# Down projection in scaled float16 pairs but for its last two rows, the sums of w_down taken under the output projection, seven PSUM banks in turn

## The chip, the cores and the metric

The kernel runs on one core of a Trainium2 chip. The metric is the device time of one execution in microseconds. A profiled execution gives a trace beside it: for each engine (PE is TensorE, PEld its weight loads, DVE is VectorE, ACT is ScalarE, POOL is GpSimd, SP is SyncE, which issues most DMAs) when each instruction ran, what it waited for, and what the DMA queues moved.

## The reference, cut to what matters

One decoder layer: modulation, a combined input projection, attention with forget gates beside a short gated convolution, an output projection, and a feed-forward part with a causal convolution of three taps. The end of it is what the change touches:

```python
x = x + g1 * (mixed @ w_out)
h2 = rmsnorm(x, norm2_g) * (1 + sc2) + sh2
u = causal_dwconv(h2 @ w_up, ffn_conv_w)
u_gate, u_val = jnp.split(u, 2, axis=-1)
y = (jax.nn.silu(u_gate) * u_val) @ w_down
return x + g2 * y
```

The sequence has 2048 tokens, the model width is 1024, the feed-forward width 2816, which is 22 rows of 128. All inputs and the output are float32.

## The kernel before

A float32 product is made as three products of pairs: each operand is split into a high part and a remainder, and high x high, high x low and low x high are added up in a PSUM bank of 512 columns (`mm3`, line 142). In the attention's end, the output projection and the up projection the parts are float16 of values that were first scaled by a power of two; in the input projection and the down projection they are f32r, a float32 with a shortened mantissa, and no scale is needed.

The stages that matter here, in order of time:

- **Output projection** (`mixed`). 64 steps n = 8 b + i: four blocks Q of 512 tokens, two column halves hf each, eight rows i of `w_out`. `prepare` makes the float16 pairs some steps ahead: a weight pair wp (in the first block) and a pair mp of the mixed activations, each with a scaled copy on ACT (line 778) and a remainder on DVE (779). At a block's first half each mp frees the buffer `src` of its raw tile, and `load_mixed` queues the load of the next block's tile into it on SP. A half block ends with four DVE readouts (826), which add x and free the four accumulator banks. A second chain, `early`, is run one piece per step under steps 17 and up, but for the last of each eight: `norm2` of blocks 0 and 1 (squares on ACT, 1108; the inverse root and the scaling on DVE, 1111 to 1115; then per column four PE transposes into the one bank of `ps_n`, line 1091, which ACT reads out, 1093, with pairs and differences after it), and then the weights of the first up row.
- **Up projection** (`up`), two halves of 1024 tokens, 22 rows i each. A row is a Strassen-like scheme of seven products of 12 matmuls (line 1250) in three banks X, Y, Z: X with o11; Y with os2; X with o12; Z with os1; Y with os3; Z with os4; Y with o22. X after o11 is copied to p1 on ACT (1295). DVE makes u2 = p1 + Y after os2 and u3 = p1 + Y after os3 (1156); the next product into Y may not start before the sum has read it. `up_weights(i + 1)` loads the next weights, scales both tiles on ACT (1176) and makes their differences and pairs. `finish`, called `last` one row later, makes the three taps of the convolution (one on ACT, 1258, two on DVE, 1263), silu (1272) and the gated product (1275), which goes to DRAM as `y_sc`.
- **Down projection** (`down`), also once per half: for each of four blocks n (token block and column half) 22 rows i. `load_pair` brings 512 columns of y and of `w_down` into one raw tile of 1024 columns, `split_pair` makes hi on ACT (1221) and lo on DVE (1222), two to three rows ahead of PE. The last two rows are multiplied together per token tile, and four readouts (1067, 1068) close the block. The four accumulators come from `ps_d`, which has four banks; `ps_u` has three more and `ps_n` one. In the first half `down` also runs `last`, `norm2` of blocks 2 and 3 and the first weights of the second up stage as a side chain, every second row.

`K(...)` pins instructions to the order in which the code issues them, and each engine works strictly in that order; PE, DVE, ACT and SP each have their own. SP's queue holds the loads in program order, so a load whose buffer is not free yet keeps back those behind it.

Of the kernel before, what the change touches and what calls it, by code (L numbers as in the profile page):

```python
# [9 lines left out]
F32 = mybir.dt.float32  # L10
# [30 lines left out]
LINES = 528  # L41
NTEMP = 7


@with_exitstack
def kernel(
# [679 lines left out]
    def halves(tiles):  # L726

        return [[t[:, n * 512 : (n + 1) * 512] for t in tiles] for n in range(2)]
# [4 lines left out]
    def load_out(n):  # L733
# [10 lines left out]
        )  # L744

    def out_scales(pool):
# [12 lines left out]
        K(T.matmul(pt[:, 0:2], lhsT=ones[0:2, :], rhs=gm, start=True, stop=True))  # L759
        bits = osc.bitcast(I32)  # L760
        K(V.tensor_scalar(osc, pt[:, 0:2], 2.0**-40, 2.0**60, op0=ALU.max, op1=ALU.min))
        K(V.tensor_scalar(bits, bits, 0x7F800000, None, op0=ALU.bitwise_and))
        K(V.reciprocal(osc, osc))
        K(V.tensor_scalar(bits, bits, 0x7F800000, None, op0=ALU.bitwise_and))
        K(V.tensor_scalar(osc, osc, 16384.0, None, op0=ALU.mult))
        K(V.tensor_tensor(oinv, osc[:, 0:1], osc[:, 1:2], op=ALU.mult))
        K(V.reciprocal(oinv, oinv))
        yield
# [284 lines left out]
    with ExitStack() as ph:  # L1053
# [10 lines left out]
        def add_gated(acc, gate, src, dst):  # L1064

            g = temp()
            K(V.tensor_tensor(g, acc, gate, op=ALU.mult))  # L1067
            K(V.tensor_tensor(src, src, g, op=ALU.add))
            nc.sync.dma_start(dst, src)

        bt = {}

# [23 lines left out]
        def norm2(Q):  # L1096

            if Q == 0:
                fp.tile([P, 96], F32, name="rim2")
            ss = fp.tile([P, 16], F32, tag="ss", name="ss", bufs=2)[:, 0:4]  # L1100
# [117 lines left out]

        def split_pair(raw):
            hi, lo = pair_tiles()  # L1220
            K(A.activation(hi, raw, AF.Copy))  # L1221
            K(V.tensor_tensor(lo, raw, hi.bitcast(F32), op=ALU.subtract))  # L1222
            y, wd = halves((hi, lo))
            return (*y, *wd)

        raws, pairs = {}, {}

        def first_pairs(hv):

            for i in range(3):  # L1230
                raws[4 * hv, i] = load_pair(4 * hv, i)
            yield
            for i in range(3):
                pairs[4 * hv, i] = split_pair(raws.pop((4 * hv, i)))
                yield
            while True:
                yield

        def up(hv):
# [25 lines left out]
            def finish(i, p1, Y, gate, val, yg):  # L1265
# [14 lines left out]
            last = None  # L1280
            for i in range(NPAIR):
                o11, o12, os2, os4, os3, o22, os1 = ops
# [12 lines left out]
                K(A.activation(p1, X, AF.Copy))  # L1295
                if last:
# [25 lines left out]
                keep_halo(gate, i)  # L1322
                next(wts)
                product(Y, o22, "t4", False)
                last = finish(i, p1, Y, gate, val, yg)
            return last

        def down(hv, side):

            todo = [(n, i) for n in range(4 * hv, 4 * hv + 4) for i in range(NPAIR)]  # L1330
            loaded = split = 3
            for e, (n, i) in enumerate(todo):
                Q, n0 = n // 2, n % 2 * 512
                rows = [slice((Q * 4 + t) * P, (Q * 4 + t + 1) * P) for t in range(4)]
                while split < min(e + 3, len(todo)):
                    if loaded == split:
                        raws[todo[loaded]] = load_pair(*todo[loaded])
                        loaded += 1
                    pairs[todo[split]] = split_pair(raws.pop(todo[split]))
                    split += 1  # L1340
# [24 lines left out]
        weights = first_weights()  # L1365
        early = chain(steps[0], (None for _ in range(1)), steps[1], weights)
        for n, _ in enumerate(mix, 8):
            if n >= 17 and n % 8 != 7:
                next(early, None)
# [33 lines left out]
```

## Time and profile before

| what | us |
|---|---|
| timed runs, median of 3 (2454.68 to 2456.41) | 2456.35 |
| the profiled execution's own time | 2452.39 |
| its span, first to last instruction | 2450.4 |
| PE busy in the span | 2361.1 (96%) |
| DVE busy | 1782.4 (73%) |
| ACT busy | 1257.3 (51%) |
| POOL busy | 361.3 (15%) |

Reading it: the mean granted TensorE clock of the span is 0.995. A matmul's length in the trace is modelled and overlaps the next one's, so the spacing of a run of matmuls (time over count) tells their rate, and the lengths of single ones don't. Shares of busy time are means over stages with different limits; the stages are looked at one by one.

### The profile page before, as it was taken

What the parts mean: (1) busy time and instruction counts of PE and PEld (TensorE: products, weight loads), DVE (VectorE), ACT (ScalarE), POOL (GpSimd) and SP (SyncE); (2) the same over time, 40 slices, a digit from 0 to 9 for tenths busy, and PEclk for the clock granted to TensorE, in tenths of its full rate; (3) what the DMA queues carried; (4) which work ended last, traced back from release to release, by engine and by line L of the source; (5) the groups of instructions that cost most, each with busy time, mean ns of one, the idle gap of its engine ahead of it and who ended that gap; (6) DMA issues with size and microseconds to landing.
All of it is one profiled execution on the core that took longest, in us unless ns stands there. A gap on an engine that the chain in (4) does not pass through costs nothing.

```text
span 2450.4 us, 38339 instructions
## 1 busy us (share of the span) xinstructions
PE 2361.1 (96%) x14419; PEld 1586.0 (65%) x14419; DVE 1782.4 (73%) x3325; ACT 1257.3 (51%) x2016; POOL 361.3 (15%) x302
## 2 busy tenths in 40 slices
PE   4999999999899888999999999999999999999999
PEld 4988788888677666444444444688864444448887
DVE  7567884442799888556888889757768888885554
ACT  3533453221588887343656565555545556554333
POOL 4210111101567785001000000000000000000000
PEclk9999999999999999999999999999999999999999
DMA  8435686543599987524222222676742222236775
GB/s 241 148 119 128 173 243 191 158 134 95 117 183 174 218 166 160 185 104 155 78 86 87 86 86 76 202 240 226 230 145 80 93 86 86 86 103 211 228 228 184
DMA packets 428707, 368.70 MB, mean 150 GB/s; under 512 B 184209, under 2 KB 327913, under 8 KB 427497
## 3 DMA queue, kind: packets, MB, share of 16 engines
q1 hardware_dynamic: 421400, 349.40, 50.4%
q10 hardware_dynamic: 4752, 8.46, 1.0%
q0 software_dynamic: 2368, 8.39, 0.9%
q8 instruction: 113, 1.85, 0.3%
q14 instruction: 74, 0.60, 0.1%
HBM read 267.54 MB, written 65.08 MB: 136 GB/s over the span
## 4 chain that ended last, share of the span: by engine, by line
PE 79%; DVE 7%; issue 5%; DMA 4%; ACT 3%; POOL 2%; SPq 1%; ACTq 0%; DVEq 0%; POOLq 0%
PE acc L1250 33%; PE acc L142 26%; PE pr L142 11%; PE pv L142 2%; DMA far<-wide 2%; PE pt L934 1%; DVE near L941 1%; PE ps L873 1%; DVE s_t L897 1%; PE ps L874 1%; PE po L970 1%; DVE acc L235 1%; PE po L972 1%; PE po L971 1%; POOL wide L926 1%
## 5 line engine op out<-in xcount | busy, mean ns | idle before, releaser
L1250 PEld LDWEIGHTS <-pair 128*128 128x128 f16 x3696 | 361.6, 98 | 436.1 <-issue 0.3
L1250 PE MATMUL acc<-t,pair 128*128 128x512 f16 x2112 | 477.4, 379 | 0.0
L1250 PE MATMUL acc<-b,pair 128*128 128x512 f16 x1584 | 363.4, 379 | 0.0
L1222 DVE TENSOR_TENSOR lo<-raw,hi 128x1024 fp32r<-128x1024 f32 x176 | 212.0, 1223 | 153.8 <-ACT hi L1221 153.5
L142 PE MATMUL acc<-hi 128*128 128x512 f32 x704 | 276.8, 393 | 1.6 <-DVE t L1067 1.6
L142 PE MATMUL acc<-lo,hi 128*128 128x512 f32 x704 | 274.3, 390 | 0.5 <-DVE lo L1222 0.5
L142 PE MATMUL acc<-hi,lo 128*128 128x512 f32 x704 | 274.1, 389 | 0.0
L1221 ACT ACTIVATE hi<-raw 128x1024 fp32r<-128x1024 f32 x176 | 182.3, 1055 | 178.7 <-PE acc L142 137.8
L1263 DVE SCALAR_TENSOR_TENSOR w<-w,fcw,w 128x1024 f32<-128x1024 f32 x176 | 226.2, 1285 | 34.6 <-ACT w L1258 25.3
L1074 ACT ACTIVATE pair<-raw 128x1024 f16<-128x1024 f32 x132 | 138.3, 1048 | 68.5 <-DVE raw L1157 68.5
L142 PE MATMUL acc<-wp,mp 128*128 128x512 f16 x768 | 171.1, 382 | 1.0 <-DVE raw L826 1.0
L1258 ACT ACTIVATE w<-w,fcw 128x1024 f32<-128x1024 f32 x88 | 100.7, 1144 | 130.6 <-DVE w L1156 130.6
L914 ACT ACTIVATE s_t<-s_t,nb,cst 128x2048 f32<-128x2048 f32 (+15 forms) x128 | 164.7, 1288 | 5.2 <-ACT nb L911 0.4
L1077 DVE TENSOR_TENSOR pair<-raw,pair 128x1024 f16<-128x1024 f32 x132 | 160.9, 1219 | 4.7 <-ACT pair L1074 4.7
L142 PE MATMUL pr<-hh,wh 128*128 128x512 f32 x384 | 153.3, 399 | 0.0
L142 PEld LDWEIGHTS acc<-hi 128*128 128x128 f32 x704 | 132.2, 188 | 31.3 <-DVE t L1067 4.4
L605 ACT ACTIVATE wx<-wx 128x512 f32<-128x512 f32 x88 | 55.6, 632 | 187.4 <-DMA wx<-in_w_up_dram 163.0
L142 PE MATMUL pr<-hl,wh 128*128 128x512 f32 x384 | 151.0, 393 | 0.0
L142 PE MATMUL pr<-hh,wl 128*128 128x512 f32 x384 | 150.7, 392 | 0.0
L142 PEld LDWEIGHTS acc<-hi,lo 128*128 128x128 f32 x704 | 132.1, 188 | 27.9
L142 PEld LDWEIGHTS acc<-lo,hi 128*128 128x128 f32 x704 | 132.2, 188 | 27.7 <-DVE lo L1222 1.1
L926 POOL TENSOR_TENSOR wide<-s_t,wide 128x1024 f16<-128x1024 f32 x64 | 136.8, 2137 | 5.3
(298 smaller groups left out, 4711.8 us busy)
## 6 DMA issues: line engine op xcount, KB each, us to landing
raw<-in_w_up_dram SPq DMA_DIRECT2D x88, 512.0 KB, 3.7
raw<-y_sc SPq DMA_DIRECT2D x176, 256.0 KB, 4.0
raw<-in_w_down_dram SPq DMA_DIRECT2D x176, 256.0 KB, 5.6
wx<-in_w_up_dram SPq DMA_DIRECT2D x88, 256.0 KB, 2.9
y_sc<-w SPq DMA_DIRECT2D x44, 512.0 KB, 2.6
wm<-in_w_ada_dram SPq DMA_DIRECT2D x128, 128.0 KB, 2.9
wr<-in_w_in_dram SPq DMA_DIRECT2D x40, 256.0 KB, 3.4
x_t<-in_x_dram SPq DMA_DIRECT2D x16, 512.0 KB, 5.4
```

What stands on the lines that cost most here:

```text
L142: ins = T.matmul(acc, lhsT=a, rhs=b, start=st, stop=sp)
L235: K(V.scalar_tensor_tensor(a, wa[:, k, :], cact[:, k : k + 1], a, op0=ALU.mult, op1=ALU.add))
L605: K(A.activation(t, t, AF.Abs, accum_out=l1[:, n : n + 1]))
L914: K(A.activation(cols, cols, AF.Exp, bias=nb[:, p : p + 1], scale=qk[:, 4:5], accum_out=un["l"][:, p : p + 1]))
L926: K(G.tensor_tensor(wide[:, 1, :], s_t[:, WB * P : WU], wide[:, 0, :], op=ALU.subtract))
L1074: K(A.activation(hi, raw, AF.Copy))
L1077: K(V.tensor_tensor(lo, raw, hi, op=ALU.subtract))
L1221: K(A.activation(hi, raw, AF.Copy))
L1222: K(V.tensor_tensor(lo, raw, hi.bitcast(F32), op=ALU.subtract))
L1250: K(T.matmul(acc, lhsT=a, rhs=b, start=st, stop=sp, skip_group_check=True))
L1258: K(A.activation(y, u[:, 0:1024], AF.Copy, scale=fcw[:, ct : ct + 1]))
L1263: K(V.scalar_tensor_tensor(y, u[:, m : m + 1024], fcw[:, m * 44 + ct : m * 44 + ct + 1], y, op0=ALU.mult, op1=ALU.add))
```

## The change

Lines are those of the program after the change where code is new, and of before in the rows of before.

1. The down projection's pairs become float16 for the first 20 of 22 rows (`LAST = 20`). y and w_down get one scale each, a power of two from their largest sums, and the readout multiplies by the inverse. The last two rows stay f32r, since y's scale must be known before their values are.

```diff
+        def split_pair(e, i, raw):
+            scales = big["rim"][:, 46:48]
+            if i < LAST:
+                t = fq.tile([P, 2048], F16, tag=("hi", "lo")[e % 2], name="yw", bufs=4)
+                parts = [[t[:, (2 * n + m) * 512 : (2 * n + m + 1) * 512] for m in range(2)] for n in range(2)]
+            else:
+                parts = halves(pair_tiles())
+            for n, (hi, lo) in enumerate(parts):
+                half, sc = raw[:, n * 512 : (n + 1) * 512], scales[:, n : n + 1]
+                K(A.activation(hi, half, AF.Copy, scale=sc))
+                K(V.scalar_tensor_tensor(lo, half, sc, hi if i < LAST else hi.bitcast(F32), op0=ALU.mult, op1=ALU.subtract))
+            return (*parts[0], *parts[1])
...
-            K(V.tensor_tensor(g, acc, gate, op=ALU.mult))
+            K(V.scalar_tensor_tensor(g, acc, big["rim"][:, 48:49], gate, op0=ALU.mult, op1=ALU.mult))
```

2. Largest sums of w_down: 22 loads of 128x1024 on SP and 22 sums of absolute values on ACT, one of each per two steps of the output projection, the sum one step behind its load. They take the two buffers `first`, which the first up weights used. Largest sums of y: one sum on ACT per up row below 20, one row later.

```diff
+        def weight_sums(i):
+            t = fp.tile([P, 1024], F32, tag="first", name="wd", bufs=2)
+            K(nc.sync.dma_start(t, w_down[i * P : (i + 1) * P, :]))
+            return lambda: K(A.activation(t, t, AF.Abs, accum_out=big["rim"][:, 20 + i : 21 + i]))
...
         for n, _ in enumerate(mix, 8):
+            if sums_of:
+                sums_of.pop()()
+            if n % 2 and 9 <= n < 9 + 2 * NPAIR:
+                if n == 9:
+                    big["rim"] = fp.tile([P, 96], F32, name="rim2")
+                sums_of.append(weight_sums((n - 9) // 2))
...
+                if i < LAST:
+                    junk = fp.tile([P, D], BF16, tag="t2", name="junk", bufs=NTEMP)
+                    mags.append(lambda: K(A.activation(junk, yv, AF.Abs, accum_out=big["rim"][:, i : i + 1])))
```

3. The scales are made in the last up row, in `first_pairs`: two DVE reductions, a PE transpose, two small DVE steps, a PE matmul and seven small DVE steps (`powers_of_two`, which `out_scales` now calls too). Two pairs instead of three are split before the down projection starts. In every up row p1's copy is now issued ahead of the next weights' scaling.

```diff
                 product(X, o11, "b11", True)
+                p1 = temp()
+                K(A.activation(p1, X, AF.Copy))
                 wts = up_weights(i + 1) if i + 1 < NPAIR else first_pairs(hv)
                 ops = next(wts)
-                p1 = temp()
-                K(A.activation(p1, X, AF.Copy))
...
-            for i in range(3):
-                pairs[4 * hv, i] = split_pair(raws.pop((4 * hv, i)))
+            K(V.tensor_reduce(om[:, 0:1], rim[:, 0:LAST], axis=AX.X, op=ALU.max))
+            K(V.tensor_reduce(om[:, 1:2], rim[:, 20 : 20 + NPAIR], axis=AX.X, op=ALU.max))
+            yield
+            pt = ps_n.tile([P, 512], F32, tag="n", name="pt")
+            K(T.transpose(pt[0:2, 0:P], om, ident))
...
+            K(T.matmul(pt[:, 0:2], lhsT=ones[0:2, :], rhs=gm, start=True, stop=True))
+            powers_of_two(pt[:, 0:2], sc, inv)
...
+            for i in range(2):
+                pairs[4 * hv, i] = split_pair(i, i, raws.pop((4 * hv, i)))
```

4. The accumulators of the down projection go round seven banks, the four of `ps_d` and the three of `ps_u`.

```diff
-                    acc = [ps_d.tile([P, 512], F32, tag="d", name="acc") for _ in range(4)]
+                    acc = []
+                    for c in range(16 * hv + 4 * (n - 4 * hv), 16 * hv + 4 * (n - 4 * hv) + 4):
+                        low_bank = (c - 16 * hv) % 7 < 4
+                        acc.append((ps_d if low_bank else ps_u).tile([P, 512], F32, tag="d" if low_bank else "u", name="acc"))
```

What this moves, as the built programs have it. First ACT in the middle of an up stage, one row before (pair is a weight pair, raw the next weights, t<-acc is p1, w<-w,fcw a first tap, the last row silu):

```order
L1074 ACTIVATE pair<-raw 128x1024
L1258 ACTIVATE w_16384<-w_16300,fcw 128x1024
L1254 ACTIVATE halo<-w_16300 128x2
L1074 ACTIVATE pair<-raw 128x1024
L1176 ACTIVATE raw<-raw,cst 128x1024 x2
L1295 ACTIVATE t_16435<-acc 128x512
L1258 ACTIVATE w_16437<-w_16301,fcw 128x1024
L1254 ACTIVATE halo<-w_16301 128x2
L1272 ACTIVATE w_16384<-w_16384 128x1024
```

And the same place after the change (junk,rim is the sum of y):

```order
L1079 ACTIVATE pair<-raw 128x1024
L1288 ACTIVATE w_16759<-w_16674,fcw 128x1024
L1284 ACTIVATE halo<-w_16674 128x2
L1308 ACTIVATE junk,rim_13660<-w_16668 128x1024
L1079 ACTIVATE pair<-raw 128x1024
L1327 ACTIVATE t_16796<-acc 128x512
L1179 ACTIVATE raw<-raw,cst 128x1024 x2
L1288 ACTIVATE w_16813<-w_16675,fcw 128x1024
L1284 ACTIVATE halo<-w_16675 128x2
L1302 ACTIVATE w_16759<-w_16759 128x1024
```

The two scalings (raw) stood ahead of p1 and the tap of val; now they stand between the two. DVE's and PE's orders inside an up row are as before.

Second, ACT in the output projection, at the start of the third block (steps 28 to 36): mp is the copy of a mixed tile, junk,ss a square of the second norm, t<-pt the readout of transposes. Before:

```order
L1093 ACTIVATE t_14093<-pt,sh_137,a_136 128x512
L1074 ACTIVATE b_14095<-t_14093 128x512
L778 ACTIVATE mp<-src,rim 128x512 x3
L1108 ACTIVATE junk,ss<-w_13819 128x1024
L1108 ACTIVATE junk,ss<-w_13820 128x1024
L778 ACTIVATE mp<-src,rim 128x512
L1108 ACTIVATE junk,ss<-w_13821 128x1024
L1108 ACTIVATE junk,ss<-w_13822 128x1024
L778 ACTIVATE mp<-src,rim 128x512 x2
L1093 ACTIVATE t_14266<-pt,sh_137,a_136 128x512
```

After, where wd,rim is a sum of w_down:

```order
L783 ACTIVATE mp<-src,rim 128x512
L1242 ACTIVATE wd,rim_13660<-wd 128x1024
L783 ACTIVATE mp<-src,rim 128x512 x2
L1242 ACTIVATE wd,rim_13660<-wd 128x1024
L1111 ACTIVATE junk,ss<-w_13833 128x1024
L1111 ACTIVATE junk,ss<-w_13834 128x1024
L783 ACTIVATE mp<-src,rim 128x512
L1111 ACTIVATE junk,ss<-w_13835 128x1024
L1111 ACTIVATE junk,ss<-w_13836 128x1024
L783 ACTIVATE mp<-src,rim 128x512
L1242 ACTIVATE wd,rim_13660<-wd 128x1024
L783 ACTIVATE mp<-src,rim 128x512
```

These are the 11th, 12th and 13th sums; the 14th follows the last row, ahead of the readout t. Each stands ahead of copies, squares or a readout that had nothing in front of them.

Third, SP's queue of the same steps after the change (src are the mixed tiles of the last block, raw x of the third):

```order
L778 DMA src<-m_cv_75 128x512
L778 DMA src<-m_cv_76 128x512
L1241 DMA wd<-in_w_down_dram 128x1024
L778 DMA src<-m_cv_77 128x512
L778 DMA src<-m_cv_78 128x512
L1241 DMA wd<-in_w_down_dram 128x1024
L778 DMA src<-m_at_71 128x512
L778 DMA src<-m_at_72 128x512
L1241 DMA wd<-in_w_down_dram 128x1024
L778 DMA src<-m_at_73 128x512
L816 DMA raw<-in_x_dram 128x1024 x4
L778 DMA src<-m_at_74 128x512
```

Before, the src and x loads stood there in the same order with nothing between them. The three wd rows are the 11th to the 13th load, and the 14th comes after the last row: each is now queued behind src loads, which wait for a mixed tile's remainder on DVE.

More of the change, by code (lines that the diff above doesn't have):

```diff
@@ L744, in load_out, with powers_of_two @@
         )
+    def powers_of_two(src, s, inv):
+        bits = s.bitcast(I32)
+        K(V.tensor_scalar(s, src, 2.0**-40, 2.0**60, op0=ALU.max, op1=ALU.min))
+        K(V.tensor_scalar(bits, bits, 0x7F800000, None, op0=ALU.bitwise_and))
+        K(V.reciprocal(s, s))
+        K(V.tensor_scalar(bits, bits, 0x7F800000, None, op0=ALU.bitwise_and))
+        K(V.tensor_scalar(s, s, 16384.0, None, op0=ALU.mult))
+        K(V.tensor_tensor(inv, s[:, 0:1], s[:, 1:2], op=ALU.mult))
+        K(V.reciprocal(inv, inv))
     def out_scales(pool):
@@ L1232, in first_pairs @@
             yield
-            for i in range(3):
-                pairs[4 * hv, i] = split_pair(raws.pop((4 * hv, i)))
+            pt = ps_n.tile([P, 512], F32, tag="n", name="pt")
+            K(T.transpose(pt[0:2, 0:P], om, ident))
+            K(V.tensor_reduce(gm[:, 0:1], pt[0:2, 0:P], axis=AX.X, op=ALU.max))
+            K(V.tensor_scalar(gm, ident[0:2, 0:2], gm[:, 0:1], None, op0=ALU.mult))
+            yield
+            pt = ps_n.tile([P, 512], F32, tag="n", name="pt")
+            K(T.matmul(pt[:, 0:2], lhsT=ones[0:2, :], rhs=gm, start=True, stop=True))
@@ L1323, in up @@
                 next(wts)
+                while mags:
+                    mags.pop(0)()
                 product(Y, o22, "t4", False)
@@ L1338, in down @@
                         loaded += 1
-                    pairs[todo[split]] = split_pair(raws.pop(todo[split]))
+                    pairs[todo[split]] = split_pair(split, todo[split][1], raws.pop(todo[split]))
                     split += 1
```

28 lines of the change are left out of this document (10 added, 18 removed).

## The prediction

> **What bounds the kernel now.** I read the page's chain first, then the stages one by one (busy time per stretch), then the chain in order of time for the rate of the matmuls, and last the timelines of the engines that feed them.
>
> ```profile
> PE 79%; DVE 7%; issue 5%; DMA 4%; ACT 3%; POOL 2%; SPq 1%; ACTq 0%; DVEq 0%; POOLq 0%
> ...
> 974.00:1157.10 183.10, 178.02 (x951) 86.93 (x948) 102.73 (x175) 75.94 (x117) 10.01 (x19) 0.99 0.44 149
> 1157.10:1555.60 398.50, 398.50 (x1848) 180.62 (x1846) 347.27 (x388) 233.13 (x346) 0.90 (x2) 1.00 0.28 89
> 1555.60:1807.40 251.80, 249.70 (x1123) 203.95 (x1122) 174.00 (x214) 131.20 (x156) 0.00 (x0) 1.00 0.71 229
> 1807.40:2206.20 398.80, 398.80 (x1850) 180.89 (x1848) 348.25 (x390) 228.09 (x302) 0.00 (x0) 1.00 0.27 88
> 2206.20:2450.40 244.20, 239.48 (x1057) 197.95 (x1055) 130.31 (x123) 91.11 (x87) 0.00 (x0) 1.00 0.67 213
> ```
>
> The rows are output projection, first up, first down, second up, second down. The second number is the stretch, then busy PE, PEld, DVE, ACT, POOL, the granted clock, DMA share and GB/s. TensorE (PE) sets the end in all five. In both up stages it never pauses, but DVE is busy 87% (347.27 of 398.50): an order that makes DVE late there is paid by PE.
>
> ```profile
> 1157.13 398.86 PE acc L1250 x1848
> 2206.30 235.32 PE acc L142 x1038
> ```
>
> This is the chain in order of time. Float16 products run unbroken at 398.86/1848 = 215.8 ns each, the f32 ones of the second down stage at 235.32/1038 = 226.7 ns. The 379 and 390 ns of the page's groups are modelled lengths of overlapping matmuls; the spacing is the price.
>
> **The change part by part. The down products: a gain of 20.9 us.** 20 of 22 rows become float16: 8 blocks x 20 x 4 x 3 = 1920 matmuls, each 10.9 ns nearer to the next. The 192 of the last two rows keep 226.7.
>
> [...]
>
> **Seven banks: a gain of 4 us.**
>
> ```profile
> 1680.29 0.61 DVE t L1067
> 1681.53 0.69 DVE t L1067
> 1682.86 0.69 DVE t L1067
> 1684.18 0.69 DVE t L1067
> ```
>
> The first down stage takes 251.8 us for 1056 matmuls at 226.7 ns (239.4) and 16 groups of four transposes at 0.44 us from one group's start to the next matmul (7.0; rows of such a group stand below): 5.4 us are left over. At the changes of column block the chain hangs on the four readouts of the accumulators (L1067), as in these rows, while PE has four banks. With seven, a block's first three banks are not those of the block before it. The second stage has no such loss (its x1038 stand unbroken), so nothing is gained there. Bounds 0 and 5.4; I take 4, since the chain rows name the banks for most of it.
>
> **Splitting the pairs: a loss of 4 us.**
>
> ```profile
> L1222 DVE TENSOR_TENSOR lo<-raw,hi 128x1024 fp32r<-128x1024 f32 x176 | 212.0, 1223 | 153.8 <-ACT hi L1221 153.5
> L779 DVE SCALAR_TENSOR_TENSOR mp<-src,rim,mp 128x512 f16<-128x512 f32 x31 | 22.7, 749 | 11.1 <-ACT mp L778 11.0
> ```
>
> One DVE subtraction of 1223 ns becomes two of the second kind, 1.41 us for two in a row (row at 1062.44 below): about 0.2 us more a pair. It is hidden while DVE has room. The first down stage is crowded (174.00 busy of 251.80, plus 88 x 0.2, in 15 us less): 1.5 us, from 0 to 5. At each change from up to down the scale adds a chain: DVE reduction, PE transpose, DVE, PE matmul, seven small DVE steps, then the split, with two pairs ready instead of three. PE waits some 0.5 us for its small matmul, and the third to fifth split reach DVE behind two taps of 2.6 us (rows below), about 0.9 us late: 1.4 us, twice, less what lookahead returns: 2.5 us, from 0 to 6.
>
> **The copy moved ahead of the weight scaling: a loss of 20 us.** One cycle of the second up stage, ACT, DVE and PE:
>
> ```profile
> 2006.70 2.75 PE L1250 MATMUL acc<-b,pair 128*128 128x512 f16 x12
> 2007.10 2.17 ACT L1176 ACTIVATE raw<-raw,cst 128x1024 f32<-128x1024 f32 x2
> 2009.49 0.60 ACT L1295 ACTIVATE t<-acc 128x512 f32<-128x512 f32 x1 [0.22 <-PE acc L1250]
> 2009.99 1.14 ACT L1258 ACTIVATE w<-w,fcw 128x1024 f32<-128x1024 f32 x1
> 2011.16 2.61 DVE L1263 SCALAR_TENSOR_TENSOR w<-w,fcw,w 128x1024 f32<-128x1024 f32 x2 [0.54 <-ACT w L1258]
> 2013.68 0.68 DVE L1156 TENSOR_TENSOR t<-t,acc 128x512 f32<-128x512 f32 x1
> 2019.94 0.68 DVE L1156 TENSOR_TENSOR t<-t,acc 128x512 f32<-128x512 f32 x1
> 2022.24 2.75 PE L1250 MATMUL acc<-t,pair 128*128 128x512 f16 x12
> ```
>
> Today ACT scales the two weight tiles (2.17 us) while it would only wait for product X, then copies X (p1, 2009.49), then makes val's first tap (2009.99), for which DVE waits (0.54). After the change p1 still starts at 2009.49, since PE sets it; the scaling comes behind it and the tap behind that: 2.08 us later, 2012.07 to 2013.21. DVE's two taps start at 2013.24 instead of 2011.16, u2 at 2015.76, which is in time for product os3. From u2 to u3 DVE runs without an outside wait (2013.68 to 2019.94, 6.26 us), so u3 stands at 2022.02 and ends at 2022.70. The product o22 (2022.24) writes the bank that u3 reads and waits for it: 0.46 us and a release, 0.5. The path starts at X's end, so it recurs each cycle. It needs a `last` and a next weight tile: rows 1 to 20, twice: 40 x 0.5 = 20 us; were DVE to close the 0.5, 0. The added sum on ACT (1.04 us, row below) falls before p1, where ACT idled or scaled, and costs nothing here.
>
> **w_down's sums under the output projection: a loss of 13.2 us.** Per piece one 512 KB load on SP's queue, and one sum on ACT:
>
> ```profile
> 1019.37 1.04 ACT L1108 ACTIVATE junk<-raw 128x1024 bf16<-128x1024 f32 x1
> ...
> raw<-in_x_dram SPq DMA_DIRECT2D x8, 512.0 KB, 6.9
> ...
> y_sc<-w SPq DMA_DIRECT2D x44, 512.0 KB, 2.6
> ...
> 1060.19 0.32 SPq L773 DMA_DIRECT2D src<-m_cv  x1
> ...
> 1061.70 1.93 ACT L778 ACTIVATE mp<-src,rim 128x512 f16<-128x512 f32 x3
> ...
> 1062.44 1.41 DVE L779 SCALAR_TENSOR_TENSOR mp<-src,rim,mp 128x512 f16<-128x512 f32 x2
> 1063.77 2.72 DVE L826 SCALAR_TENSOR_TENSOR w<-acc,rim,w 128x512 f32<-128x512 f32 x4
> ...
> 1060.15 18.29 PE L142 MATMUL acc<-wp,mp 128*128 128x512 f16 x84
> ```
>
> 22 x 1.04 us would fit into ACT's 107 idle us. But ACT works in order, and a sum waits for its load. The 11th load stands on SP behind the m_cv load of 1060.19, so it is issued at about 1060.6; 512 KB take between 2.6 and 6.9 us to land, I take 3.9 beside other loads: 1064.5. ACT reaches the 11th sum at 1062.3, waits, and ends at 1065.6. Behind it stands the copy of a mixed tile (mp), behind that DVE's remainder, and behind that the four readouts of 1063.77 that free the banks: the first ends at about 1067.7, while PE wants it at 1065.33 (24 matmuls after 1060.15): **2.4 us**.
>
> ```profile
> 1070.74 0.16 DVE L1111 TENSOR_SCALAR ss<-ss 128x4 f32<-128x4 f32 x1
> ...
> 1075.11 1.41 DVE L1115 TENSOR_SCALAR w<-w,ss 128x1024 f32<-128x1024 f32 x2
> ...
> 1078.28 0.60 PE L1091 MATMUL pt<-ident,w 128*128 128x128 f32 x4
> 1078.72 2.75 PE L142 MATMUL acc<-wp,mp 128*128 128x512 f16 x12
> 1081.31 0.60 PE L1091 MATMUL pt<-ident,w 128*128 128x128 f32 x4
> ```
>
> The 12th load waits on SP for that remainder (issued at 1067.4, landed at about 1071.5), its sum ends at 1072.5, and only then come the squares of the second norm: 4.1 us for four, two copies of 0.7 among them, the 5.8 us from 1070.74 to the last scaled tile, and one more remainder (0.7) in DVE's way: 1084.5. PE's transposes come due at 1080.7 (1078.28 + 2.4): **3.8 us**. The 14th load stands behind four loads of x that leave near 1080 (6.9 us), so its sum holds ACT until about 1090. The second group of transposes follows the first by 3.0 us (1078.28 to 1081.31), comes due at 1087.5, and needs the bank that ACT reads only after that sum: **3.3 us**. The fifth sum holds up the first norm the same way; its tiles now are ready at 1028 (1025.25 + 2.74) for 1034.85, and its load stands among x loads and the stores of x1: 0 to 3.3, and I take half, **1.7 us**.
>
> ```profile
> 1025.25 2.74 DVE L1115 TENSOR_SCALAR raw<-raw,ss 128x1024 f32<-128x1024 f32 x4
> ...
> 1034.85 0.60 PE L1091 MATMUL pt<-ident,raw 128*128 128x128 f32 x4
> ...
> 1107.29 0.66 PE L1091 MATMUL pt<-ident,w 128*128 128x128 f32 x4 [2.17 <-ACT t L1093]
> 1107.79 14.80 PE L142 MATMUL acc<-wp,mp 128*128 128x512 f16 x60
> ...
> 1107.80:1111.80 4.00, 4.00 (x13) 1.50 (x11) 3.81 (x7) 2.69 (x5) 0.00 (x0) 0.57 0.44 131
> ```
>
> A pause also costs clock: after the 2.17 us before 1107.29 the granted clock was 0.57 for 4 us, and 60 matmuls took 14.80 us instead of 13.1, a loss of 1.7. I add **2.0** for four pauses of 2 to 3.5 us (0 to 6.8). [...] Together 13.2; bounds 0 (every load landed in time) and 24 (6.9 us a load, all pauses throttled).
>
> **Sum:** -20.9 - 4 + 1.5 + 2.5 + 20 + 13.2 = +12.3 us on the profiled execution's 2452.39 (span 2450.4 and 2.0 around it). The three timed runs have their median 4.0 us higher, 2456.35; I add to that: **2468.6**.
>
> **The rivals.**
> 1. *The sums find their loads landed* (for it: DMA is only 44% busy there; against: the loads stand behind others on SP): minus 13.2, 2455.4, no change.
> 2. *DVE keeps its time in the up stages*, place and price as above. It decides at 0.5 us: if the path from X to u3 is that much shorter, o22 never waits and 20 us go: 2448.6, **faster** by 0.3%. Against it: the cycle's rows show no outside wait to absorb it.
> 3. *Both covers hold*: 2435.4.
> 4. *Loads land late and every pause is throttled*: +10.8, 2479.4. For it: 229 GB/s already in the first down stage, loads of 6.9 us.
> 5. *The change brings no faster products*: float16 in this stage at 226.7 ns: +20.9, 2489.5. Against it: the unbroken float16 products of both up stages. [...]
>
> **How the numbers follow.** Forecast 0.50, rivals 0.20, 0.12, 0.05, 0.10, 0.03. About 0.2% (4.9 us) is what a measurement of this kernel can tell from no change. Faster: rivals 2 and 3 and an edge of 1, 0.20. Same: most of rival 1 and the low edge of the forecast, 0.22. Slower: 0.58. Cases of both signs are near; the forecast's own range is 2461 to 2477, and with rivals 1, 2 and 4 and the open sizes the range is 2447 to 2482.
>
> **What will show it.** Down: chain pieces of float16 acc at 215.8 ns, both stages some 10 to 15 us shorter. Up: a DVE wait of about 0.5 us before the o22 products, the stretches near 409 instead of 399; at 399 that step was wrong. Output projection: near 196 instead of 183, with ACT idle for DMA wd before the sums; at 183 that step was wrong.

## The result, and the profile after

| | us |
|---|---|
| before, median of 4 timed runs (2454.68 to 2456.41) | 2456.14 |
| after, median of 4 timed runs (2481.42 to 2485.84) | 2484.27 |
| ratio after/before, 95% interval | 1.0115, [1.0103, 1.0128] |
| profiled execution after, and its span | 2484.69, 2483.0 |

The change makes the kernel 28.1 us slower. The forecast had the direction, 2468.6 against 2484.27, and its range ended 2.3 us too low.

The stages of the kernel after, as the prediction showed those of before (output projection, first up, first down, second up, second down; columns as there):

```profile
978.20:1182.30 204.10, 185.04 (x951) 88.49 (x948) 103.07 (x175) 96.81 (x159) 9.88 (x19) 0.96 0.57 190
1182.30:1591.50 409.20, 402.46 (x1852) 180.82 (x1851) 344.51 (x397) 254.00 (x387) 1.03 (x2) 1.00 0.27 85
1591.50:1838.50 247.00, 238.88 (x1122) 118.80 (x1120) 191.68 (x303) 153.43 (x243) 0.00 (x0) 1.00 0.73 237
1838.50:2247.70 409.20, 402.47 (x1851) 180.77 (x1851) 345.53 (x399) 248.84 (x343) 0.00 (x0) 1.00 0.26 84
2247.70:2483.00 235.30, 229.70 (x1058) 111.66 (x1056) 149.29 (x212) 117.38 (x176) 0.00 (x0) 0.99 0.68 225
```

Against before: output projection 183.1 to 204.1 (+21.0), the up stages 398.5 and 398.8 to 409.2 each (+21.1 together), first down 251.8 to 247.0 (-4.8), second down 244.2 to 235.3 (-8.9). That is +28.4. The span grew by 32.6; the other 4.2 lie ahead of 978.20, where the change alters no work. That part scatters between executions: in the traces of the experiments below, the first product of the output projection starts 1.2 to 6.2 us later than in before, and after the change 4.2 us later. The profiled execution of before happened to be short (2452.39 where its timed runs have 2456.14), that of after was not.

The page's shares of the chain that ended last say the same in one line. Before, PE had 79% of it and DVE 7%:

```profile
PE 50%; DVE 23%; ACT 10%; issue 8%; DMA 7%; POOL 2%; SPq 0%; ACTq 0%; DVEq 0%; POOLq 0%
```

A stage in which PE never waits is one PE piece in that chain. The first up stage was one (398.86 us, x1848). The chain in order of time for one row of it after the change:

```profile
1235.08 5.36 PE acc L1280 x24
1240.46 0.50 ACT t L1327
1240.96 2.17 ACT raw L1179 x2
1243.13 1.05 ACT w L1288
1244.20 1.30 DVE w L1293
...
1253.05 0.61 DVE t L1159
...
1253.70 5.36 PE acc L1280 x24
```

From one PE row to the next it is 18.62 us (1235.08 to 1253.70); seven products of 12 unbroken matmuls need 84 x 215.8 ns = 18.13. The chain leaves PE at X, goes through p1 (L1327), both scalings (L1179) and the tap (L1288) on ACT, then through DVE, whose own work fills the left-out pieces, to u3 (the last L1159), on which o22 waits. It is the forecast's path, with its 0.49 us a row.

### The profile page after: what moved, and what is told of

Same layout as the page of the kernel before. It is cut to its first block, busy times and chain, and to the rows that moved or that the text cites. A ratio compares the mean times of both kernels' runs of the same rounds, so it can differ in the third digit from the quotient of the medians.

```text
span 2483.0 us, 38909 instructions
## 1 busy us (share of the span) xinstructions
PE 2356.1 (95%) x14425; PEld 1416.3 (57%) x14425; DVE 1813.6 (73%) x3523; ACT 1368.3 (55%) x2316; POOL 360.9 (15%) x302
## 4 chain that ended last, share of the span: by engine, by line
PE 50%; DVE 23%; ACT 10%; issue 8%; DMA 7%; POOL 2%; SPq 0%; ACTq 0%; DVEq 0%; POOLq 0%
PE acc L143 20%; PE pr L143 11%; PE acc L1280 10%; ACT raw L1179 3%; DVE raw L1160 3%; DVE t L1159 3%; DMA far<-wide 3%; DVE pair L1082 3%; DVE w L1293 3%; PE pv L143 2%; ACT w L1288 2%; DVE w L1305 2%; DMA wd<-in_w_down_dram 1%; DVE yw L1233 1%; PE pt L939 1%
## 5 line engine op out<-in xcount | busy, mean ns | idle before, releaser
L1280 PE MATMUL acc<-t,pair 128*128 128x512 f16 x2112 | 477.3, 379 | 13.2 <-DVE t L1159 13.2
L143 PE MATMUL acc<-yw 128*128 128x512 f16 x1920 | 420.1, 379 | 7.6 <-DVE yw L1233 4.6
L143 PEld LDWEIGHTS <-yw 128*128 128x128 f16 x1920 | 187.2, 98 | 233.8 <-issue 11.2
L1233 DVE SCALAR_TENSOR_TENSOR yw<-raw,rim,yw 128x512 f16<-128x512 f32 x320 | 221.3, 746 | 63.5 <-ACT yw L1232 63.0
L1232 ACT ACTIVATE yw<-raw,rim 128x512 f16<-128x512 f32 x320 | 208.9, 711 | 88.1 <-DMA raw<-y_sc 42.2
L1288 ACT ACTIVATE w<-w,fcw 128x1024 f32<-128x1024 f32 x88 | 100.5, 1142 | 84.6 <-DVE w L1159 84.6
L902 DVE CUSTOM_DVE_ANT_0 s_t<-ps,nf,mx 128x512 f32<-128x512 f32 (+1 forms) x192 | 119.3, 643 | 15.8 <-PE ps L881 7.5
L143 PEld LDWEIGHTS <-mp 128*128 128x128 f16 x768 | 76.5, 100 | 93.9 <-issue 10.6
L878 PE MATMUL ps<-kh,qs 128*128 128x512 f16 (+1 forms) x320 | 109.8, 347 | 6.7 <-DVE mx L902 5.7
L946 DVE TENSOR_TENSOR near<-pt,near 128x512 f16<-128x512 f32 (+1 forms) x192 | 101.2, 551 | 15.5 <-ACT near L941 14.9
```

The lines of the kernel that those rows point to most:

```text
L143: ins = T.matmul(acc, lhsT=a, rhs=b, start=st, stop=sp)
L878: K(T.matmul(ps[:, 0:cw], lhsT=qt, rhs=kh[:, c0 : c0 + cw], start=True, stop=False))
L902: K(V.tensor_tensor_reduce(out=s_t[:, o0 + c0 : o0 + c0 + cw], in0=ps[:, 0:cw], in1=nf[:, c0 : c0 + cw], scale=1.0, scalar=-3.0e38 if g == ...
L1232: K(A.activation(hi, half, AF.Copy, scale=sc))
L1233: K(V.scalar_tensor_tensor(lo, half, sc, hi if i < LAST else hi.bitcast(F32), op0=ALU.mult, op1=ALU.subtract))
L1280: K(T.matmul(acc, lhsT=a, rhs=b, start=st, stop=sp, skip_group_check=True))
```

## The experiments

All times are medians; after is 2484.27 us, and before, measured again beside the experiments, took 2454.06 to 2455.68.

**One part undone at a time.** The copy of p1 behind the scaling again:

```diff
-                p1 = temp()
-                K(A.activation(p1, X, AF.Copy))
                 wts = up_weights(i + 1) if i + 1 < NPAIR else first_pairs(hv)
                 ops = next(wts)
+                p1 = temp()
+                K(A.activation(p1, X, AF.Copy))
```

> The changed kernel, but p1's copy stands behind the weight scaling again, as before; y's sums stay on ACT. Theory (the tap of val is 2.08 us late, so u3 keeps product o22 waiting 0.49 us in 40 rows): both up stages return from 409.4 to 398.7 us and the time falls by 20 to 22 us, to about 2463. Rival (the added sums of y, 1.04 us of ACT in 40 rows, lengthen the rows): the up stages stay near 409 and the time near 2484.

Measured: 2464.0 us (ratio to before 1.004 [1.0023, 1.0058]), 20.3 less. Its first up stage (the second has the same 399.50):

```profile
1179.60:1579.10 399.50, 399.39 (x1852) 181.09 (x1851) 346.54 (x397) 250.30 (x385) 1.00 (x2) 1.00 0.27 87
```

PE is busy throughout again, 9.7 us a stage less than after the change. ACT does nearly the same work as there (250.30 against 254.00 us); only the order differs.

Loads and sums of w_down left out:

```diff
                 if n == 9:
                     big["rim"] = fp.tile([P, 96], F32, name="rim2")
-                sums_of.append(weight_sums((n - 9) // 2))
+                    K(V.memset(big["rim"][:, 20 : 20 + NPAIR], 16.0))
```

> The changed kernel without w_down's loads and sums under the output projection; a constant stands for their result. Theory (the output projection is 21.2 us longer because of them): it returns from 187.6 to about 166.5 us and the time falls to about 2463. Rival (those 21 us are a delay brought in by other edits, such as the buffers first that the first up weights shared): it stays above 180 us.

Measured: 2461.89 us (1.0029 [1.0018, 1.0039]), 22.4 less; its output projection, counted from the same point, takes 183.0 us instead of 204.1.

Four banks again:

```diff
-                    acc = []
-                    for c in range(16 * hv + 4 * (n - 4 * hv), 16 * hv + 4 * (n - 4 * hv) + 4):
-                        low_bank = (c - 16 * hv) % 7 < 4
...
+                    acc = [ps_d.tile([P, 512], F32, tag="d", name="acc") for _ in range(4)]
```

> The changed kernel with four banks in the down projection. Theory (seven banks hide the readouts in the first down stage alone): the first down stage grows from 246.9 by 2 to 4 us, the second stays at 235.0 within 0.5. Rival (the waits at the block changes were DVE's lateness with the pairs, which banks don't touch): no change in either.

Measured: 2489.17 us (2486.39 to 2490.55), 4.9 more, of which its trace shows 1.9 in the first down stage (248.9 us) and nothing in the second. Runs of one kernel spread by 4 us, so the banks are worth 2 to 5 us.

All 22 rows in f32r pairs, scaled:

```diff
-            if i < LAST:
+            if i < 0:
                 t = fq.tile([P, 2048], F16, tag=("hi", "lo")[e % 2], name="yw", bufs=4)
...
-                K(V.scalar_tensor_tensor(lo, half, sc, hi if i < LAST else hi.bitcast(F32), op0=ALU.mult, op1=ALU.subtract))
+                K(V.scalar_tensor_tensor(lo, half, sc, hi.bitcast(F32), op0=ALU.mult, op1=ALU.subtract))
```

> The changed kernel with scaled f32r pairs in all 22 rows, four instructions a pair as in the change, all else kept. Theory (float16 gives 10.9 ns for each of 1920 matmuls, 10.4 us a stage): the second down stage with its tail grows from 235.0 to about 245, and the first by less than 10.4, since DVE and ACT with their late pairs set part of its time: 3 to 8 us. Rival (the float16 products give their full 10.4 us in both stages and the loss in the first is from something else): both grow by 10.

Measured: 2500.3 us (2498.62 to 2501.24), 16.0 more. Its two down stages:

```profile
1590.20:1844.50 254.30, 250.68 (x1122) 203.86 (x1120) 192.37 (x303) 154.42 (x243) 0.00 (x0) 1.00 0.71 230
2253.80:2498.90 245.10, 240.08 (x1058) 198.13 (x1056) 150.15 (x212) 117.48 (x176) 0.00 (x0) 0.99 0.68 216
```

The second gains 9.8 us by float16 (245.1 to 235.3), nearly all of the 10.45 that half the forecast term says. The first gains 7.3: the faster products run into something else there.

**Why the sums cost 22 us.** ACT's busy time in the stage rises by 20.9 us (75.94 to 96.81), and it sat idle for 107 us there before, so the work itself should fit. Two kernels take the coupling apart. The loads alone, nobody waiting for them:

```diff
-            return lambda: K(A.activation(t, t, AF.Abs, accum_out=big["rim"][:, 20 + i : 21 + i]))
+            return lambda: None
...
+                    K(V.memset(big["rim"][:, 20 : 20 + NPAIR], 16.0))
```

> The 22 loads of w_down stay under the output projection, the 22 sums on ACT are left out and a constant stands in their place, so the scale of w_down is not measured. Theory (the cost of 22.4 us that leaving both out took away comes from ACT standing in order at a sum whose load has not landed, with the evictions and norm copies behind it): without the sums nobody waits for these loads, the output projection falls from 187.6 us to 166-172 and the time to 2461-2468. Rival A (the transfers themselves delay the loads of the next quarter's operands and the stores of x1): the stage keeps 180 us or more, time 2476 or more. Rival B (the buffers of the loads hold up the sync queue): as A, with the waits of the sync queue at the load's buffer.

And the sums alone, all over one tile:

```diff
-            t = fp.tile([P, 1024], F32, tag="first", name="wd", bufs=2)
-            K(nc.sync.dma_start(t, w_down[i * P : (i + 1) * P, :]))
+            if i == 0:
+                big["wd"] = fp.tile([P, 1024], F32, tag="first", name="wd", bufs=2)
+                K(nc.sync.dma_start(big["wd"], w_down[i * P : (i + 1) * P, :]))
+            t = big["wd"]
```

> The 22 sums stay on ACT, but all over one tile that is loaded once, so that only the first waits for a load; the scale of w_down comes from its first 128 rows alone. Theory (waiting for the loads, not the work, is the cost): the work is 22 times about 1.2 us of ACT = 26 us in a stage in which ACT has idle time; output projection 168-175 us, time 2462-2471. Rival (ACT's own work delays the evictions as much): the stage stays at 183 us or more, time 2479 or more. If this kernel and the one with the loads alone both come near the kernel without either, the cost lies in the coupling of the two; if one of them keeps the most of it, that one is the cause.

Measured: 2463.22 us (ratio to before 1.0032 [1.0019, 1.0046]) and 2464.37 us (1.0035 [1.0023, 1.0046]). The output projection of each, loads alone first:

```profile
978.40:1161.40 183.00, 177.94 (x952) 87.01 (x949) 102.68 (x176) 73.88 (x115) 9.91 (x19) 0.99 0.62 212
```

```profile
978.40:1161.60 183.20, 178.07 (x950) 86.81 (x947) 102.88 (x175) 96.07 (x159) 9.86 (x19) 0.99 0.46 152
```

Each half by itself is free in this stage. The loads move the same bytes as after the change in a shorter stage (212 GB/s against 190), and nobody loses by it; the sums keep ACT busy for 96.07 us, as after the change (96.81), and nobody loses by that. Slow loads as such are not the cause either. These two rows are the issues of w_down's loads over the output projection, after the change and with the loads alone (last column: median us from issue to landing).

```profile
wd<-in_w_down_dram SPq DMA_DIRECT2D x22, 512.0 KB, 6.5
```

```profile
wd<-in_w_down_dram SPq DMA_DIRECT2D x22, 512.0 KB, 9.3
```

They land later where they cost nothing. What costs is the ring that the two close together, to be read in the chain of the kernel after:

```profile
1070.79 0.68 DVE mp L784
1071.49 0.33 SPq L778
1071.87 4.38 DMA wd<-in_w_down_dram
1076.27 1.15 ACT wd L1242 x2
1077.41 0.62 ACT mp L783
1078.06 0.76 DVE mp L784
1078.84 0.32 SPq L778
1079.21 4.86 DMA wd<-in_w_down_dram
...
1088.74 0.32 SPq L778
1089.11 4.50 DMA wd<-in_w_down_dram
```

DVE's remainder of a mixed tile frees its `src` buffer; only then may SP issue the next src load, and behind it the load of w_down; ACT stands at the sum until that lands; behind the sum stands the copy of the next mixed tile, and DVE's remainder waits for that copy. One turn takes 7.35 us (1071.49 to 1078.84), the next 9.90 (to 1088.74). The kernel takes one such load per two steps of the projection, 24 matmuls, which PE does in 5.2 us (24 x 215.8 ns). So the ring falls behind PE with each turn, and PE waits. With the loads alone ACT does not wait for them, with the sums alone SP has nothing in its queue that ACT waits for, and both runs are free of the cost. That the sums also hold back the next loads can be read from the times at which the 11th to the 14th load of w_down are issued: 7.3, 9.9 and 7.8 us apart after the change (1071.87 to 1096.92), and 3.6, 4.8 and 7.1 us apart with the loads alone (1065.02 to 1080.59). So the two runs show that the coupling of load and sum costs the 21 us, and the form of it, the ring, is read from the chain and these times. No run kept both and took only the link on SP away. Eight of the 22 sums waited for their load at all, 45.8 us together.

**Why the first down stage gained so little.** In before PE waited there 2.1 us for DVE (1.6 for readouts, 0.5 for a pair). After, these are PE's waits in it:

```profile
PE acc L143 <- DVE yw L1233: 4.0, 7, 1.0
PE acc L143 <- ACT yw L1232: 2.6, 2, 1.6
PE acc L143 <- ACT hi L1232: 0.9, 1, 0.9
```

The pairs come late. Splitting five rows ahead instead of three:

```diff
-                while split < min(e + 3, len(todo)):
+                while split < min(e + 5, len(todo)):
```

> Splitting runs five rows ahead of the products in both down stages instead of three. Theory (the first down stage gained 4.75 us instead of the forecast 11.7 because its pairs come late: PE waits some 10 us for scaled pairs while ACT stands in order at the second norm's copies): the first down stage falls from 246.9 us to 239-243, the second stays at 235, time 2476-2481. Rival (ACT and DVE are simply full there, a longer lead is used up within a few rows): first down stage 245-248, time 2483-2487.

Measured: 2489.0 us, slower, with 248.4 us in the first down stage and 238.8 in the second. Neither theory had that. The lead over the products was bought with the lead of the loads over the splits: the loads stay six rows ahead of the products, and so only one row ahead of the splits instead of three. These are the splits on ACT in the first down stage, after the change and in this kernel (idle time before them, and for what):

```profile
L1232 ACT ACTIVATE yw<-raw,rim 128x512 f16<-128x512 f32 x158 | 101.3, 708 | 11.3 <-DMA raw<-y_sc 9.0 <-DMA raw<-in_w_down_dram 1.1 <-DVE yw L1233 0.9
```

```profile
L1232 ACT ACTIVATE yw<-raw,rim 128x512 f16<-128x512 f32 x158 | 102.4, 709 | 36.6 <-DMA raw<-y_sc 32.8 <-DMA raw<-in_w_down_dram 1.9 <-PE acc L143 1.4
```

What this did to PE is not plain waiting. In the first down stage PE waited 7.4 us in all, no more than the 7.8 after the change, but in longer pieces (up to 2.1 us against 1.6). At a mean granted clock of 0.99 against 1.00, PE was busy 240.93 us with the same matmuls instead of 238.88. In the second stage PE waited 2.6 us instead of 0.6 and was busy 231.25 us instead of 229.70.

So the loads were moved too, once with the splits and once alone:

```diff
-                while loaded < min(e + 6, len(todo)):
+                while loaded < min(e + 9, len(todo)):
```

> Loads of the down stages are issued up to nine rows ahead (four buffers) and splitting runs five rows ahead. With splitting alone moved ahead, ACT's waits for the loads of y in the first down stage rose from 9.0 to 32.8 us and the stages grew by 1.6 and 3.5 us. Theory (the splits lack a lead over the products, and the loads lacked a lead over the splits): with both, first down stage 238-243 us instead of 246.9, second 233-236, time 2476-2481. Rival (the queue of loads has no room: DMA is busy 0.73 of this stage, and an earlier issue lands no earlier; four raw buffers limit it): first down 246-249, second 235-239, time 2484-2490.

> Loads of the down stages issued up to nine rows ahead, splitting three rows ahead as in the change. Theory (of the some 10 us that PE waits for pairs in the first down stage a part starts with loads: ACT waits 9.0 us for loads of y, 5.5 us of it in one piece at 1605-1610 us): 2-5 us less in the first down stage, 242-245 us, time 2479-2483. Rival (the loads are not the limit, ACT stands at the second norm's copies with the splits behind it): first down 246-248 us, time 2483-2486.

Measured: both ahead 2479.48 us (2474.91 to 2485.58), 4.8 less, with 242.4 us in the first down stage, 0.9 us of waits for pairs left there (and 2.7 for tiles of the second norm), and 234.4 in the second. The loads alone ahead: 2511.19 us, 26.9 **more**, with 273.6 us in the first down stage. I had not thought of that case. These are waits in that stage of the last kernel, first of SP's queue, then of ACT and PE:

```profile
SPq L1218 <- DVE yw L1233: 127.7, 75, 9.0
```

```profile
ACT junk L1111 <- DMA w<-x_sc: 17.4, 2, 8.8
PE acc L143 <- DVE yw L1233: 17.6, 6, 6.1
```

After the change these three are 103.7, 5.2 and 4.0 us; with both ahead, where the stage got shorter, they are 111.7, 10.5 and 0.5. So SP's long wait by itself says little, and what stands out is PE's. It looks like the ring of the output projection in another place. There are four raw buffers, and loads six rows ahead of the splits fill them, so SP's queue stands at a load until a later split frees a buffer. The loads of x for the second norm (w<-x_sc) are queued behind it, ACT stands in order at the squares that need them, and the split is behind those on ACT. With loads four rows ahead of the splits, as many as there are buffers, the same move pays. That the loss comes from this ring is read from the waits; no kernel took it apart. Of the 26.6 us in this stage 8.1 are not waits but PE's busy time, 246.99 us against 238.88, at a mean granted clock of 0.96 against 1.00.

**A version that beats both.** The copy back, and the sums moved to where nothing feeds back: into the rows of the first up stage, each sum one row (18 us) behind its load.

```diff
                     K(A.activation(u[:, 0:2], halo[:, ct, :], AF.Copy))
+                if hv == 0:
+                    while sums_of:
+                        sums_of.pop(0)()
+                    for _ in range(0 if i in (0, 20, 21) else 2 if i in (5, 10, 15) else 1):
+                        sums_of.append(weight_sums(len(summed)))
+                        summed.append(i)
                 product(Y, os2, "t2", True)
...
-                sums_of.append(weight_sums((n - 9) // 2))
```

The first such kernel also split five rows ahead, before the result of that step alone was known:

> A version put together from the findings: the copy of p1 is back behind the scaling of the next row's weights, splitting runs five rows ahead, and w_down's loads and sums are moved out of the output projection into the rows of the first up stage, each sum one row (18 us) behind its load. Theory: 20.3 us (the copy) and 22.4 us (the sums) less than the change, and nothing paid in the up rows since ACT waits there about 1.5 us a row for the accumulators anyway and no load is late: first up 399-401 us, output projection 166-168, time 2434-2443. Rival (22 more sums of 1.2 us in the rows of the first up stage delay the gate's readout and the tap, 0.5 us or more a row): first up 409-425, time 2450-2468.

Measured: 2447.95 us (0.9963 [0.9947, 0.9979] of before), with 399.3 us in the first up stage, 250.5 in the first down stage and 238.8 in the second. The up rows took the sums for nothing; the gap to the theory lies in the down stages, with the step that lost 4.7 us by itself. Without it:

> The copy of p1 back behind the scaling, and w_down's loads and sums in the rows of the first up stage; splitting three rows ahead as in the change. Theory: the version that also split five rows ahead lost 3.4 us in the first down stage and 3.6 us in the second by it; without that, output projection 164-167 us, both up stages 399-400, first down 247, second 235, time 2438-2444, faster than the kernel before by 11-17 us. Rival (the sums in the up rows moved something that makes the down stages longer, the split ahead not being the cause): first down 249-251, second 238-239, time 2446-2450.

Measured: 2442.55 us, 0.995 [0.9934, 0.9967], faster than before, as the theory had it; its first down stage takes 246.7 us and its second 235.2, so the split ahead alone had been the cause. And with loads and splits ahead:

> All findings together: the copy of p1 behind the scaling, w_down's sums in the rows of the first up stage, loads up to nine rows and splitting five rows ahead in the down stages. Theory (the three costs lie in different stages and add): from the version without the longer leads (2442.55 us) the first down stage 246.5 to 242 us and the second 235.0 to 234: time 2436-2439, 15-18 us under the kernel before. Rival (the leads make something late at the transition from up to down, where the up rows now run 10 us shorter a stage): first down 246 us or more, time 2442 or more.

Measured: 2438.9 us (2433.55 to 2444.1), **0.9938 [0.9924, 0.9953]** of before. Its stages:

```profile
975.40:1158.40 183.00, 177.93 (x954) 86.94 (x951) 102.81 (x175) 75.96 (x117) 9.87 (x18) 0.99 0.44 149
1158.40:1557.80 399.40, 399.29 (x1852) 181.00 (x1850) 346.42 (x397) 272.54 (x429) 1.08 (x2) 1.00 0.36 116
1557.80:1802.50 244.70, 240.27 (x1122) 119.80 (x1120) 191.03 (x303) 155.44 (x245) 0.00 (x0) 0.99 0.74 239
...
2201.90:2436.40 234.50, 229.57 (x1059) 111.75 (x1056) 148.86 (x212) 116.25 (x176) 0.00 (x0) 1.00 0.69 226
```

The first up stage carries 22 loads and sums more (ACT 272.54 us, and 250.30 with the copy put back alone) and still takes 399.4 us. The first down stage came to 244.7 instead of the expected 242. Of the 2.3 us by which it is longer than with the leads alone, 1.5 are PE's busy time (240.27 against 238.80 us, both at a mean granted clock of 0.99). The timed difference between the last two versions, 3.7 us, is no more than the spread of their runs.

## Why the prediction was right about the direction and low by 15.7 us

The stages of the two profiled executions differ by 28.4 us, the timed medians by 28.1. By the terms of the sum:

| term | forecast | measured in the traces | from |
|---|---|---|---|
| copy of p1 ahead of the scaling | +20 | +19.4 (timed 20.3) | up stages; copy put back |
| rest of the up stages | 0 | +1.7 | 399.5 against 398.5 and 398.8 |
| sums under the output projection | +13.2 | +21.0 (timed 22.4) | stage; sums left out |
| float16 down products | -20.9 | -17.1 (timed 16.0) | against f32r pairs |
| seven banks | -4 | -1.9 (timed 4.9) | against four banks |
| splitting, both stages | +4 | +5.3 | the rest of -13.7 in the down stages |

**Right:** the copy. The step was a path added up row by row in one cycle (tap 2.08 us later, DVE without a break to u3, 0.5 us a row), and chain, row period (0.49 us longer) and the kernel with the copy put back agree with it. The rival "DVE keeps its time" fell with that. The rate of the float16 products is right as well: after the change the chain's long piece in the second down stage is

```profile
2259.34 214.64 PE acc L143 x989
```

217.0 ns a matmul, the 215.8 of float16 with the last two rows' 226.7 among them.

**Wrong in size, the step on w_down's sums.** The mechanism (ACT in order at a sum, its load on SP behind others) was the right one, and the places were right: first norm, evictions behind the 11th sum, second norm, ps_n bank. It is the sizes that failed, 11.2 us for the pauses and 2.0 for the clock (its four pauses, called 2 to 3.5 us there, are 1.7 to 3.8 by its own terms). PE's waits in this stage after the change, for what, in all, times and longest:

```profile
PE pt L1096 <- ACT t L1098: 8.3, 3, 4.1
PE acc L143 <- DVE w L831: 2.7, 1, 2.7
PE pt L1096 <- DVE raw L1118: 2.6, 4, 1.6
PE pt L1096 <- DVE w L1118: 2.3, 3, 1.7
PE pt L1096 <- DMA src<-m_at: 2.0, 1, 2.0
```

That is 17.9 us, where before had 4.0 (3.0 for the readout of transposes, 1.0 for evictions): 13.9 more instead of 11.2. Place by place, less what before waited there: evictions behind the 11th sum 1.7 us (forecast 2.4), the first transposes of the second norm 4.3 (3.8), the ps_n bank behind the 14th sum 4.1 (3.3), and the first norm 3.8, where the step took 1.7, the half of its bound. The load behind which the first norm waited took 6.76 us and not 3.9 (the median of the 22 is 6.5):

```profile
1026.16 6.76 DMA wd<-in_w_down_dram
```

The larger part of the miss, 5.0 of 7.8 us, is not waiting. PE was also busy for 7.0 us longer with the same matmuls (185.04 against 178.02 us, modelled the same way in both traces), where the step had 2.0, and most of that is the clock. The granted clock was half (0.50) in three stretches of this stage, 17.1 us in all (1043.39 to 1050.22, 1098.00 to 1101.42, 1104.83 to 1111.66), against one of 3.41 in before. In the chain, behind two of the three drops:

```profile
1046.24 9.80 PE acc L143 x36
...
1107.69 12.38 PE acc L143 x48
```

36 matmuls at 215.8 ns are 7.77 us and 48 are 10.36, so these pieces cost 2.0 us each. By an estimate, the half of PE's busy time in the three stretches (13.6 us), the clock cost 6.8, less the 1.7 that before paid as well: 5.1 instead of 2.0. That 2.0 was my choice between none and all of four times the 1.7 of before; no run shows it. Waits and clock together are 19.0 of the 21.0. The last 2.0 are busy time as well, 1.5 of it the first transposes of each norm, which came one at a time as their tiles got ready (1.3 and 1.4 us busy, where a group of four takes 0.6). The upper bound that the step named, 24 (6.9 us a load, all pauses throttled), lay nearer than the value taken.

**Wrong in size, the first down stage.** Forecast 10.45 + 4 - 2.75 = 11.7 us of gain, measured 4.8. The term that failed most is the splitting, "1.5 us" for a crowded stage, and with it the full 10.45 for float16, which counts on pairs that are ready in time. Splitting scaled pairs with no faster products already cost this stage 4.4 us (251.8 to 254.3 with seven banks, which give 1.9), and float16 then gained 7.3 instead of 10.45. The step counted DVE's extra work (0.2 us a pair) and put ACT's at nothing without a reason: a pair now takes two copies of 710 ns on ACT instead of one of 1050, 111.9 us in this stage (101.3 + 10.6) against 86.6 before, and 3.5 of PE's 7.8 us of waits name ACT. Nor did it count the lead: faster products use up three rows of lead in less time, while ACT stands in order at the second norm's copies and at loads (10.4 us for y after; before 14.3 for w_down, which came last there). No run took apart what the 4.4 are made of. The miss of 6.9 is thus 1.65 (4.4 for 2.75) + 3.15 (7.3 for 10.45) + 2.1 (the banks, 1.9 for 4). Of the first two, 4.8, longer leads of loads and splits brought back 4.6 (242.4). In the second down stage, which has no second norm beside it, forecast and measurement agree (9.2 = 10.45 - 1.25, and 8.9).

**The range** fell short because the output projection and the first down stage were both at the bad end at once. I had priced them apart, but by the waits both hang on loads that stand on one SP queue and on ACT, which waits for them in order. The float16 term, which came out 3.8 us short, had no bounds at all. The clock's part also varies between executions: six other traces with the same code in the output projection have that stage 19.8 to 23.5 us longer than before, and the mean granted clock of a whole run is 0.989 to 0.992 in the four after the change and 0.990 to 0.995 in the four with four banks.

## What to carry to other kernels

Before you add a load and its use to a stage with slack, follow the four queues once round: if the load can be held back by work that stands behind its use, it is a ring, and where one turn takes longer than the stage needs for its share of the work, the turn sets the pace (here 7 to 10 us a turn against 5.2, for 1.2 us of work on ACT). Loads alone and uses alone, two small kernels, tell whether the coupling or a shortage costs; the times at which the loads are issued then show whether the uses hold them back. Compare PE's busy time as well as its waits: of 21.0 us an estimated 5.1 were clock lost behind pauses. A lead is counted per link: lengthening one link (splits, or loads) without the next made the stage 1.4 and 26.6 us longer, and both together 4.6 us shorter.

## What the runs showed of the hardware that was not expected

The length of a pause of PE did not settle by itself whether the granted clock dropped behind it. In before, 2.17 us of waiting that ended at 1107.29 were followed by 4.00 us (1107.80 to 1111.80) at a mean granted clock of 0.57. After the change, 2.73 us that ended at 1079.53 and 2.16 us that ended at 1133.91 left the clock at 1.00 (the second number is the length of the stretch, the third PE's busy time, the third from the end the granted clock):

```profile
1079.50:1083.50 4.00, 3.98 (x19) 1.80 (x19) 2.60 (x4) 0.00 (x0) 2.11 (x4) 1.00 0.84 226
1131.00:1136.00 5.00, 2.84 (x18) 1.69 (x17) 2.94 (x5) 4.05 (x7) 0.00 (x0) 1.00 0.28 105
```

So of three pauses the longest cost no clock, and two that differ by 0.01 us went different ways. No kernel here changes a pause alone, so the runs do not tell what made the difference.
